# Block inverses of a chunked delta rule written straight into the tile of M, without mask, expansion and the intermediate W

## The chip, the cores and the metric

The kernel runs on one core of one Trainium2 chip, in float32. The metric is the device time of one execution in microseconds. The five engines are called as in the profile: PE (TensorE; its weight loads are PEld), DVE (VectorE), ACT (ScalarE), POOL (GpSimd) and SP (SyncE, which here only issues DMAs). Each works through its own list of instructions in order, and waits on semaphores for what another one has to finish first.

## The reference, cut to what matters

One encoder layer on x (1 x 2048 x 1024): a norm, one projection, then two groups that read it. Group A is a gated delta rule, forward and backward, with 4 heads of 128; group B is windowed attention. Their outputs are concatenated, projected and added to x. The change lies in group A, in the inverse of a triangular matrix per chunk:

```python
m = jnp.where(strict, jnp.einsum('bhncd,bhnsd->bhncs', k_beta, k) * decay, 0.0)
t_inv = lax.linalg.triangular_solve(eye + m, jnp.broadcast_to(eye, m.shape),
                                    left_side=True, lower=True, unit_diagonal=True)
u = jnp.einsum('bhncs,bhnse->bhnce', t_inv, v * beta[..., None])
w = jnp.einsum('bhncs,bhnsd->bhncd', t_inv, k_beta * jnp.exp(g)[..., None])
...
_, o = lax.scan(step, state0, xs)          # chunk after chunk, forwards
bwd = flip(gated_delta_rule_chunked(flip(q), flip(k), flip(v), ...))
```

The reference uses chunks of 64; the kernel uses 16 chunks of 128, which gives the same function. So each of the 4 heads has 2 directions x 16 chunks = 32 inverses of a unit triangular 128x128 matrix.

## The kernel before, in words

Phase A (to about 840 us) makes the projections, the convolution and the attention and leaves its results in DRAM. Phase B does group A head by head, and both output projections. For a head h it has these parts:

- `pre_front(h)`: for each of four groups `c4` of four chunks it loads keys and queries (`kq`), transposes them (`tr`), multiplies them (`gh`, two products of 256 columns per chunk), and DVE scales the products by decay (`dc`) and beta (`bp`) into the tile `ma[d, c4]` (L666). `ma[:, c, 0]` is M of chunk c, `ma[:, c, 1]` the matrix for the queries. `ssk` and `nk` are norms of the keys: squares on ACT, then DVE, then a power on POOL (L647). M goes to DRAM (`m_d`).
- the solve, at the head of `pre_back(h)`: the 32x32 blocks on the diagonals of all 32 matrices come back as one tile `L` (128 rows = 32 matrices x 4 blocks), and DVE inverts them together in 31 steps of two operations (L701, L705), each of which needs the one before. The result X goes to DRAM (`x_d`).
- the inverses, in the loop over `hi`: four pairs, group hi of direction 0 and group 3-hi of direction 1. For each group `xc` brings the inverted blocks, one 128x32 strip per chunk. POOL spreads each strip over 128 columns and multiplies it with the 0/1 mask `blk`, which leaves the block-diagonal matrix `xd` (L716); DVE transposes it 32x32 block by block into `xt` (L720). One of them is the right side x0 of the product `pb` = M x0 (L725), the other, x1, is the start of the iteration. ACT copies the blocks of `pb` off the diagonal into B (`bm`, L731, three copies). Then three times: a product `pw` = B W on PE (L737), and W = x1 - `pw` on DVE, 128x512 (L742). The third result is written over M, in `ma[:, :, 0]`.
- `scan(h)`: 16 steps, each for both directions: `pk`, `r`, `py` (the product with the inverse in `ma`), `yk` and `y` on ACT, `po` (three products), the new state `S` and the output `oacc`. Step i of direction 0 takes chunk i, of direction 1 chunk 15-i, so the first four steps need the first pair of inverses alone. `post` then norms the outputs (`sso`, `tro`, `zt`).

The order of all this is not that of the code: `set_order` plans the whole program. It takes every instruction with a cost by engine, shape and kind and a delay from one engine to the next, plays the program forwards and backwards twelve times by list scheduling, and fixes each engine's list as in the best plan. So the solve and the inverses of head h+1, and the front of head h+2, stand between the steps of scan h. The names in the lists are those above with head, direction and group: `pb2_1_3` is `pb` of head 2, direction 1, group 3. PE's products in float32 are two instructions each.

## Time and profile before

| | us |
|---|---|
| median of 3 runs | 1356.98 (1355.6 to 1359.8) |
| profiled execution, its own time | 1359.47 |
| its span in the profile | 1357.7 |
| PE busy | 1286.7 (95%) |
| DVE busy | 945.8 (70%) |
| ACT busy | 689.1 (51%) |
| POOL busy | 414.3 (31%) |

The profiled execution is 2.5 us above the median, and its span 1.8 us below its own time. "Busy" is the time in which an instruction of the engine was under way. The matmul instructions overlap each other in the profile, since each is listed with its whole passage through the engine, so PE's 95% leaves room that only the spacing of starts shows. In the rows of groups, waits and timeline, L with a number is a line of the kernel before; "<-" behind a time names what ended the wait.

### The profile page before, as it was taken

How to read it: one execution, taken by the hardware profiler on the slowest of the kernel's cores; microseconds unless marked ns; L12 is line 12 of the kernel's file. 1: busy time of each engine (PE TensorE's matmuls, PEld its weight loads, DVE VectorE, ACT ScalarE, POOL GpSimd, SP SyncE). 2: the span in 40 equal slices, each digit the busy share in tenths (PEclk: the TensorE clock that was granted, in tenths of full speed). 3: DMA queues.
4: the chain of work that ended last, by engine and by line, in shares of the span. 5: the costliest groups of instructions: out<-in, count | busy, mean ns of one | idle time of the engine just before them, and what ended most of it. 6: DMA issues, size and time to landing. Idle time of an engine off the chain costs nothing. (4 is left out here: it accounts for less than half of the span.)

```text
span 1357.7 us, 23034 instructions
## 1 busy us (share of the span) xinstructions
PE 1286.7 (95%) x7546; PEld 1106.8 (82%) x7546; DVE 945.8 (70%) x2346; ACT 689.1 (51%) x2025; POOL 414.3 (31%) x562
## 2 busy tenths in 40 slices
PE   5999989999999999999999899999979989999998
PEld 4998778788998888888887677789868869898776
DVE  4322477774632499999997797868898979977532
ACT  6322254332433466767667876129577575465310
POOL 1330062100121246657777644014034041120000
PEclk9999999999999999999999899999999999999999
DMA  8342255244434533223333658968476383332776
GB/s 263 112 132 91 74 162 170 68 132 137 150 119 119 164 104 109 64 86 96 99 127 118 216 179 255 286 193 240 112 211 167 87 226 85 96 104 87 235 246 209
DMA packets 219831, 201.26 MB, mean 148 GB/s; under 512 B 48320, under 2 KB 170944, under 8 KB 219712
## 3 DMA queue, kind: packets, MB, share of 16 engines
q1 hardware_dynamic: 219712, 199.79, 48.5%
q8 instruction: 60, 0.98, 0.3%
q14 instruction: 59, 0.48, 0.1%
HBM read 134.66 MB, written 65.08 MB: 147 GB/s over the span
## 5 line engine op out<-in xcount | busy, mean ns | idle before, releaser
L185 PE MATMUL pf_c<-xhi,wh_c 128*128 128x512 f32 x384 | 150.6, 403 | 5.4 <-DVE acc L236 5.4
L236 DVE SCALAR_TENSOR_TENSOR acc<-pf_c,cw,acc 128x512 f32<-128x512 f32 (+1 forms) x192 | 140.1, 743 | 21.8 <-ACT acc L232 20.2
L186 PE MATMUL pf_c<-xlo,wh_c 128*128 128x512 f32 x384 | 150.3, 402 | 0.0
L187 PE MATMUL pf_c<-xhi,wl_c 128*128 128x512 f32 x384 | 148.3, 399 | 0.0
L354 POOL TENSOR_SCALAR pr<-pr,st 128x384 f32<-128x384 f32 (+1 forms) x128 | 86.3, 691 | 35.6 <-DVE st L352 23.7
L186 PE MATMUL pf_z<-xlo,wh_z 128*128 128x512 f32 x256 | 93.7, 398 | 0.0
L185 PE MATMUL pf_z<-xhi,wh_z 128*128 128x512 f32 x256 | 93.5, 398 | 0.0
L187 PE MATMUL pf_z<-xhi,wl_z 128*128 128x512 f32 x256 | 93.0, 398 | 0.0
L185 PEld LDWEIGHTS pf_c<-xhi,wh_c 128*128 128x128 f32 x384 | 72.7, 189 | 21.0 <-DVE acc L236 5.3
L345 ACT ACTIVATE pr<-pr,st 128x384 f32<-128x384 f32 (+1 forms) x128 | 76.2, 597 | 26.6 <-DVE st L344 25.3
L187 PEld LDWEIGHTS pf_c<-xhi,wl_c 128*128 128x128 f32 x384 | 72.6, 189 | 14.6
L186 PEld LDWEIGHTS pf_c<-xlo,wh_c 128*128 128x128 f32 x384 | 72.7, 190 | 13.9
L359 PE MATMUL pt<-ident,pr 128*128 128x128 f32 x368 | 73.2, 281 | 8.0 <-POOL pr L354 5.3
L340 DVE CUSTOM_DVE_ANT_0 pr<-s,mask,sink 128x384 f32<-128x384 f32 (+1 forms) x128 | 72.8, 592 | 8.4 <-PE s L339 4.9
L716 POOL TENSOR_TENSOR xd<-xc,blk 128x512 f32<-128x512 f32 x32 | 41.3, 1300 | 120.3 <-DMA xc<-x_d 59.7
L737 PE MATMUL pw<-W,bm 128*128 128x128 f32 x512 | 73.4, 280 | 0.6 <-DVE W L742 0.4
L772 ACT ACTIVATE yk<-py,ck 128x128 f32<-128x128 f32 x120 | 43.7, 364 | 58.2 <-PE py L767 57.3
L363 ACT ACTIVATE ph<-pt 128x512 fp32r<-128x512 f32 x92 | 53.5, 594 | 38.1 <-PE pt L359 27.3
L359 PEld LDWEIGHTS pt<-ident,pr 128*128 128x128 f32 x368 | 49.1, 143 | 26.9 <-POOL pr L354 11.4
L364 DVE TENSOR_TENSOR pl<-pt,ph 128x512 fp32r<-128x512 f32 x92 | 62.2, 683 | 10.6 <-ACT ph L363 9.3
L737 PEld LDWEIGHTS pw<-W,bm 128*128 128x128 f32 x512 | 65.0, 194 | 2.8 <-DVE W L742 1.6
L177 DVE TENSOR_TENSOR wl_c<-ws_c,wh_c 128x512 fp32r<-128x512 f32 x48 | 36.1, 756 | 38.4 <-ACT wh_c L176 25.7
(244 smaller groups left out, 3776.7 us busy)
## 6 DMA issues: line engine op xcount, KB each, us to landing
kqc<-kq_d SPq DMA_DIRECT2D x120, 128.0 KB, 2.6
ws_c<-wt SPq DMA_DIRECT2D x48, 256.0 KB, 3.5
xr<-x SPq DMA_DIRECT2D x16, 512.0 KB, 5.9
ws_z<-wt SPq DMA_DIRECT2D x32, 256.0 KB, 3.6
kq<-kq_d SPq DMA_DIRECT2D x16, 512.0 KB, 5.0
xrs<-x SPq DMA_DIRECT2D x32, 256.0 KB, 3.9
part<-xrs SPq DMA_DIRECT2D x32, 256.0 KB, 3.5
m_d<-ma SPq DMA_DIRECT2D x32, 256.0 KB, 4.9
```

The lines of the kernel that those rows point to most:

```text
L185: T.matmul(ps, hi[:, k, cs], xhi[b][:, k], start=(k == 0), stop=False)
L186: T.matmul(ps, hi[:, k, cs], xlo[b][:, k], start=False, stop=False)
L187: T.matmul(ps, lo[:, k, cs], xhi[b][:, k], start=False, stop=(k == KC - 1))
L236: V.scalar_tensor_tensor(av, ps[:, lo:], cw[:, i, k : k + 1], av, ALU.mult, ALU.add)
L340: V.tensor_tensor_reduce(pr[j][:, :n], ps[:, :n], mask[:, lo * P : hi * P], 1.0, sink[:, hh : hh + 1], ALU.add, ALU.max, accum_out=mx[:, j ...
L345: A.activation(pr[j][:, :n], pr[j][:, :n], AF.Exp, bias=nm[:, j : j + 1], accum_out=den[:, j : j + 1])
L354: G.tensor_scalar(pr[j][:, :n], pr[j][:, :n], den[:, j : j + 1], 1.0, ALU.mult, ALU.mult)
L359: T.transpose(pt[:, j], pr[j][:, (kb - lo) * P : (kb - lo + 1) * P], ident)
L363: A.activation(ph, ptf, AF.Copy)
L364: V.tensor_tensor(pl, ptf, ph.bitcast(F32), ALU.subtract)
L737: T.matmul(pw_[:, c], B[:, c], wt[d][:, c], start=True, stop=True)
L772: A.activation(yk, py, AF.Copy, scale=ck[:, d, c : c + 1])
```

## The change

The mask `blk`, the expanded tiles `xd` and `xt` of 128x512 per group and the tiles W are gone. In their place:

- four tiles `xz` (two per direction, like B) are set to zero once. Of a strip x0, only the three blocks that `pb` needs are copied into the diagonal of `xz`, by POOL, as three copies of 32 partitions x 4 x 32.
- DVE transposes the strip itself (128x128 per group instead of 128x512).
- ACT writes B negated (`scale=-1.0`).
- POOL copies the four diagonal blocks x1 into the tile of M, once `pb` has read M.
- the three products read that tile itself instead of W. After product k only the blocks at distance k from the diagonal are new, and only they are written back into it: three copies on ACT after product 1, two on DVE after product 2, one on DVE after product 3.

```diff
-    NXB, NW = 3, 2
     XE = V
-    blk = const("blk", [P, P], t["blk"], qp)
     bms = [[const(f"bm{d}_{i}", [P, 4, P], None, qp) for i in range(2)] for d in range(2)]
-    for grp in bms:
+    xds = [[const(f"xz{d}_{i}", [P, 4, P], None, qp) for i in range(2)] for d in range(2)]
+    for grp in bms + xds:
         for a in grp:
             G.memset(a, 0.0)
...
-                xd = qp.tile([P, 4, P], F32, tag="xd", name=f"xd{h}_{d}_{c4}", bufs=NXB)
-                xt = qp.tile([P, 4, P], F32, tag="xt", name=f"xt{h}_{d}_{c4}", bufs=NXB)
-                B = bms[d][xcount[0] // 2 % 2]
+                k = xcount[0] // 2 % 2
+                B, xd = bms[d][k], xds[d][k]
                 xcount[0] += 1
                 xc = qp.tile([P, 4, 32], F32, tag="xc", name=f"xc{h}_{d}_{c4}", bufs=3)
+                xt = qp.tile([P, 4, 32], F32, tag="xt", name=f"xt{h}_{d}_{c4}", bufs=3)
                 dma(xc, x_d[d, 4 * c4 : 4 * c4 + 4].rearrange("u i c -> i u c"))
-                G.tensor_tensor(
-                    xd.rearrange("p u (q c) -> p u q c", q=4), xc.unsqueeze(2).to_broadcast([P, 4, 4, 32]),
-                    blk.rearrange("p (q c) -> p q c", q=4).unsqueeze(1).to_broadcast([P, 4, 4, 32]), ALU.mult,
-                )
-                V.transpose(xt.rearrange("p c i -> p (c i)"), xd.rearrange("p c i -> p (c i)"))
-                prs.append((d, c4, B) + ((xd, xt) if d == 0 else (xt, xd)))
+                V.transpose(xt.rearrange("p u c -> p (u c)"), xc.rearrange("p u c -> p (u c)"))
+                x0, x1 = (xc, xt) if d == 0 else (xt, xc)
+                for q in quads[d : d + 3]:
+                    G.tensor_copy(xd[q, :, q], x0[q])
+                prs.append((d, c4, B, xd, x1))
...
-                    A.activation(B[r, :, q], pb[r, :, q], AF.Copy)
-            wt = {d: x1 for d, c4, B, x0, x1 in prs}
-            for k in range(3):
+                    A.activation(B[r, :, q], pb[r, :, q], AF.Copy, scale=-1.0)
+                for q in quads:
+                    G.tensor_copy(ma[d, c4][q, :, 0, q], x1[q])
+            for k in range(1, 4):
                 for d, c4, B, x0, x1 in prs:
+                    m = ma[d, c4]
                     pw_ = ps_i[d].tile([P, 4, P], F32, tag="inv", name=f"pw{h}_{d}_{c4}_{k}")
                     for c in range(4):
-                        T.matmul(pw_[:, c], B[:, c], wt[d][:, c], start=True, stop=True)
-                    if k < 2:
-                        wt[d] = qp.tile([P, 4, P], F32, tag="W", name=f"W{h}_{d}_{c4}_{k}", bufs=NW)
-                    else:
-                        wt[d] = ma[d, c4][:, :, 0]
-                    V.tensor_tensor(wt[d], x1, pw_, ALU.subtract)
+                        T.matmul(pw_[:, c], B[:, c], m[:, c, 0], start=True, stop=True)
+                    for p in range(4 - k):
+                        r, q = (quads[p], quads[p + k]) if d == 0 else (quads[p + k], quads[p])
+                        if k == 1:
+                            A.activation(m[r, :, 0, q], pw_[r, :, q], AF.Copy)
+                        else:
+                            V.tensor_copy(m[r, :, 0, q], pw_[r, :, q])
```

Since the plan is made anew, the lists differ far beyond these lines, on PE from the second half of phase A on. Three places, all at the passage from scan 1 to scan 2, show what moves. In the lists of after, the lines behind the change are one lower or higher (L760 is now L761, L666 is L665, L742's place is taken by L743, L725 by L723, L716 by L718 and L731).

The first is DVE's list where the solve of head 2 ends (`X2`, L705, now L704). Before:

```order
L760 SCALAR_TENSOR_TENSOR r1_0_14_11911<-pk1_0_14_11909,negc_5022,vs1_3_10933 128x128
L779 SCALAR_TENSOR_TENSOR S1_1_13_11902<-S1_1_12_11816,egt_5024,po1_1_13_11894 128x128
L795 SCALAR_TENSOR_TENSOR oacc1_3_11337<-po1_0_13_11874,egc_5026,oacc1_3_11337 128x128
L666 SCALAR_TENSOR_TENSOR ma3_1_0_13601<-gh3_0_0_13634,bp3_13429,dc3_0_1_13598 128x256
L760 SCALAR_TENSOR_TENSOR r1_1_14_11931<-pk1_1_14_11929,negc_5022,vs1_0_10855 128x128
L795 SCALAR_TENSOR_TENSOR oacc1_0_11324<-po1_1_13_11894,egc_5026,oacc1_0_11324 128x128
L796 TENSOR_TENSOR oacc1_3_11337<-po1_0_13_11874,oacc1_3_11337 128x128
L796 TENSOR_TENSOR oacc1_0_11324<-po1_1_13_11894,oacc1_0_11324 128x128
L666 SCALAR_TENSOR_TENSOR ma3_0_0_13597<-gh3_0_0_13634,bp3_13429,dc3_0_0_13594 128x256
L666 SCALAR_TENSOR_TENSOR ma3_1_0_13601<-gh3_0_0_13634,bp3_13429,dc3_0_1_13598 128x256
L779 SCALAR_TENSOR_TENSOR S1_0_14_11922<-S1_0_13_11882,egt_5024,po1_0_14_11914 128x128
L705 TENSOR_TENSOR X2_12346<-X2_12346,tm2_30_12441 128x31
```

Now:

```order
L761 SCALAR_TENSOR_TENSOR r1_0_12_11887<-pk1_0_12_11885,negc_5022,vs1_3_10987 128x128
L796 SCALAR_TENSOR_TENSOR oacc1_2_11600<-po1_0_11_11850,egc_5026,oacc1_2_11600 128x128
L797 TENSOR_TENSOR oacc1_1_11579<-po1_1_11_11870,oacc1_1_11579 128x128
L797 TENSOR_TENSOR oacc1_2_11600<-po1_0_11_11850,oacc1_2_11600 128x128
L813 TENSOR_SCALAR sso1_1_11923<-ssq1_10676 128x8
L700 TENSOR_TENSOR tm2_30_12543<-L2_12447,X2_12448 128x31
L743 COPY ma1_1_0_10847<-pw1_1_0_2_11396 32x4x32 x2
L704 TENSOR_TENSOR X2_12448<-X2_12448,tm2_30_12543 128x31
```

The last step of this solve stood behind step 14 of scan 1 and stands now behind step 11. For head 3 it went from step 11 to step 9 of scan 2, for head 1 from step 12 to step 13 of scan 0.

The second is PE's list at the first product with the inverted blocks of head 2. Before:

```order
L769 MATMUL po1_0_15_11954<-S1_0_14_11922,kqc1_0_15_11947 128x128
L785 MATMUL po1_0_15_11954<-y1_0_15_11957,ma1_0_3_10867 128x128
L769 MATMUL po1_1_15_11969<-S1_1_14_11942,kqc1_1_15_11962 128x128
L785 MATMUL po1_1_15_11969<-y1_1_15_11972,ma1_1_0_10793 128x128
L674 MATMUL trv3_3_13736<-ident_66,vt3_3_13670 128x128 x4
L657 MATMUL gh3_3_1_13723<-kq3_3_13668 128x256 x2
L725 MATMUL pb2_0_0_12457<-xd2_0_0_12445,ma2_0_0_12193 128x128 x4
L725 MATMUL pb2_1_3_12465<-xt2_1_3_12452,ma2_1_3_12275 128x128 x4
```

Now:

```order
L759 MATMUL pk1_0_14_12011<-S1_0_13_11984,kqc1_0_14_12009 128x128
L777 MATMUL po1_1_13_11996<-yk1_1_13_11999,ks1_0_10853 128x128
L786 MATMUL po1_0_13_11976<-y1_0_13_11981,ma1_0_3_10921 128x128
L723 MATMUL pb2_0_0_12561<-xz0_0_8568,ma2_0_0_12295 128x128
L768 MATMUL py1_0_14_12015<-r1_0_14_12013,ma1_0_3_10921 128x128
L723 MATMUL pb2_0_0_12561<-xz0_0_8568,ma2_0_0_12295 128x128
L759 MATMUL pk1_1_14_12031<-S1_1_13_12004,kqc1_1_14_12029 128x128
```

It stood behind the last product of scan 1; now its first half stands between the products of steps 13 and 14.

The third is POOL's list there. Before:

```order
L647 TENSOR_TENSOR nk3_13428<-ssk3_13427,pw_4992 128x4
L631 TENSOR_TENSOR dc3_3_1_13676<-dc3_3_1_13676,dmask_4984 128x512
L716 TENSOR_TENSOR xd2_0_0_12445<-xc2_0_0_12447,blk_8564 128x512
L716 TENSOR_TENSOR xd2_1_3_12451<-xc2_1_3_12453,blk_8564 128x512
L814 TENSOR_TENSOR sso1_0_11977<-sso1_0_11977,pw_4992 128x8
```

Now:

```order
L718 COPY xz0_0_8568<-xc2_0_0_12547 32x4x32 x3
L718 COPY xz1_0_8570<-xt2_1_3_12555 32x4x32 x3
L630 TENSOR_TENSOR dc3_3_0_13822<-dc3_3_0_13822,dmask_4984 128x512
L646 TENSOR_TENSOR nk3_13578<-ssk3_13577,pw_4992 128x4
L718 COPY xz0_1_8569<-xc2_0_1_12627 32x4x32 x2
L630 TENSOR_TENSOR dc3_3_1_13826<-dc3_3_1_13826,dmask_4984 128x512
L731 COPY ma2_0_0_12295<-xt2_0_0_12548 32x4x32 x4
L718 COPY xz0_1_8569<-xc2_0_1_12627 32x4x32
L731 COPY ma2_1_3_12377<-xc2_1_3_12554 32x4x32 x4
```

The last group of head 3's front (`dc3_3`, `nk3`) stood ahead of head 2's first blocks and stands now between them and the copies into the tile of M.

More of the change, by code (lines that the diff above doesn't have):

```diff
@@ L1182, in layout @@
     dmask = np.stack([np.where(le, f(0), f(NEG)), np.where(i >= j, f(0), f(NEG))], 1).astype(f)
-    blk = (i // 32 == j // 32).astype(f)
     r = {
@@ L1189, in layout @@
         "sinks": g["swa_sinks"][0], "ident": np.eye(P, dtype=f), "cs": cs, "smask": smask, "tri": tri,
-        "dmask": dmask, "blk": blk, "eye32": np.eye(32, dtype=f),
+        "dmask": dmask, "eye32": np.eye(32, dtype=f),
     }
```

## Prediction

> **What bounds the kernel now.** I read the windows by stage first, then the spacing of PE's starts in the timeline, then the timeline of one passage from scan to scan, then PE's waits. The change lies in phase B alone, between 905 us (first `pb`) and 1262 us (last scan step):
>
> ```profile
> core 0: us, PE busy (x) PEld busy (x) DVE busy (x) ACT busy (x) POOL busy (x), PEclk, DMA share, GB/s
> 905.00:1009.00 104.00, 93.99 (x702) 87.20 (x701) 88.61 (x273) 74.94 (x325) 29.82 (x25) 0.97 0.59 162
> 1028.00:1101.00 73.00, 69.05 (x536) 63.22 (x535) 66.93 (x214) 48.46 (x202) 14.59 (x13) 1.00 0.51 139
> 1123.00:1188.00 65.00, 62.66 (x492) 57.77 (x493) 61.30 (x190) 32.02 (x117) 10.74 (x8) 1.00 0.31 86
> 905.00:1262.00 357.00, 329.83 (x2540) 304.94 (x2539) 304.55 (x906) 226.60 (x914) 86.15 (x68) 0.99 0.51 140
> ```
>
> PE is busy 92% of the 357 us, DVE 85%, ACT 63%, POOL 24%. In the bodies of scans 1 and 2 (second and third row) DVE stands at 92 and 94%: two engines are nearly full side by side. How much of PE's time is work shows in its starts where nothing is late:
>
> ```profile
> 1052.41 1.06 PE L737 MATMUL pw<-W,bm 128*128 128x128 f32 x8
> 1053.31 0.39 PE L767 MATMUL py<-r,ma 128*128 128x128 f32 x2
> ...
> 1016.99 1.13 PE L657 MATMUL gh<-kq 128*128 128x256 f32 x4
> 1017.96 0.61 PE L737 MATMUL pw<-W,bm 128*128 128x128 f32 x4
> ```
>
> Eight instructions of 128 columns take 1053.31 - 1052.41 = 0.90, so 0.1125 each and 0.225 a product (two instructions); a `gh` product takes 0.97/2 = 0.485. 2540 instructions at 0.1125 make 286, and the some 92 of 256 columns add 92 x 0.13 = 12: PE has 298 us of work in 357, and loses 59. That is what can be won.
>
> **Where it is lost.** Part of it is the passage from one scan to the next. The chain is solve, DRAM and back, block matrix, `pb`, B, three products with a step on DVE between, first `py`. From scan 1 to scan 2 the timeline has:
>
> ```profile
> 1099.44 0.18 DVE L705 TENSOR_TENSOR X<-X,tm 128x31 f32<-128x31 f32 x1
> 1100.40 0.55 SPq L706 DMA_DIRECT2D x_d<-X  x1
> 1105.36 2.17 SPq L715 DMA_DIRECT2D xc<-x_d  x3
> 1108.30 2.50 POOL L716 TENSOR_TENSOR xd<-xc,blk 128x512 f32<-128x512 f32 x2 [5.75 <-DMA xc<-x_d]
> 1109.62 2.07 PE L725 MATMUL pb<-xd,ma 128*128 128x128 f32 x8 [2.13 <-POOL xd L716]
> 1111.73 1.15 ACT L731 ACTIVATE bm<-pb 32x128 f32<-32x128 f32 x3 [2.29 <-PE pb L725]
> 1121.17 0.39 PE L767 MATMUL py<-vs,ma 128*128 128x128 f32 x2
> ```
>
> So 21.6 us go by from the end of the solve (1099.6) to the first `py`. PE's list holds from `pk1_0_15`, which ran as the solve ended, to `pb2_0_0` 10 products, 5 `gh` and 7 transposes (one instruction each): 2.25 + 2.43 + 0.79 = 5.5 us; from there to `py2_0_0` 32 products and 8 transposes: 8.1. 13.6 of 21.6 are work, 8.0 are lost. The other two passages, by the same rows:
>
> ```profile
> 998.45 0.18 DVE L705 TENSOR_TENSOR X<-X,tm 128x31 f32<-128x31 f32 x1
> 1025.30 0.39 PE L767 MATMUL py<-vs,ma 128*128 128x128 f32 x2
> ...
> 1175.08 0.17 DVE L705 TENSOR_TENSOR X<-X,tm 128x31 f32<-128x31 f32 x1
> 1196.66 0.39 PE L767 MATMUL py<-vs,ma 128*128 128x128 f32 x2
> ```
>
> Scan 0 to 1: 26.7 us, in PE's list 21.7 of work, 5.0 lost. Scan 2 to 3: 21.4, 18.0 of work, 3.4 lost. The three lose 16.4. The rest is in the scans, where PE's waits name DVE and ACT about equally; idle that shows as such is less than the loss by starts, since matmuls overlap:
>
> ```profile
> PE gh L657 <- DVE ma L666: 5.3, 4, 3.0
> PE pb L725 <- POOL xd L716: 3.3, 2, 2.1
> PE tro L824 <- ACT oacc L821: 3.2, 6, 1.7
> PE tr L637 <- ACT ks L640: 2.3, 2, 1.9
> PE po L776 <- ACT yk L772: 2.3, 6, 0.6
> PE py L767 <- DVE r L760: 2.2, 6, 0.6
> ```
>
> **The change, part by part.** The rows for the prices:
>
> ```profile
> 905.00:1262.00 357.00, 65.05 (x96) 0.99 0.51 140
> ...
> L720 DVE STREAM_TRANSPOSE xt<-xd x32: 668/702/714, 901.0 to 1229.2; 128x512 f32<-128x512 f32 x32
> ...
> L783 DVE COPY S<-po x8: 248/286/291, 917.1 to 1200.5; 128x128 f32<-128x128 f32 x8
> ...
> L731 ACT ACTIVATE bm<-pb 32x128 f32<-32x128 f32 x32 | 8.6, 268 | 19.6 <-PE pb L725 18.7
> ...
> L716 POOL TENSOR_TENSOR xd<-xc,blk x32: 1262/1270/2109, 898.9 to 1216.9; 128x512 f32<-128x512 f32 x32
> ...
> L258 POOL COPY bd<-sgkv x16: 192/196/433, 31.4 to 381.5; 128x16 f32<-128x16 f32 x16
> ...
> L354 POOL TENSOR_SCALAR pr<-pr,st x128: 472/586/1803, 196.5 to 836.4; 128x384 f32<-128x384 f32 x112, 128x256 f32<-128x256 f32 x16
> ```
>
> DVE. It loses the 96 subtractions (first row, the windows of L742 alone: 65.05 us) and 32 transposes of 512 columns (22.5). It gains 32 transposes of 128 columns, which no row has: between 0.18 (a quarter) and 0.70, taken 0.28 as the copy of the same width, 9 us; and 96 copies of 128 columns from PSUM at 0.28, 27. Net 51 us less, 304.6 to 253 of 357, 71%.
>
> ACT. 96 more copies of 32x128 from PSUM at 0.268: 25.7 us, 63% to 71%. The sign in B costs nothing: the same instructions with another constant.
>
> POOL. 32 x 7 = 224 copies of 128 elements instead of 32 `xd`. A copy lies between 0.196 (16 elements) and 0.472 (fastest of 384); on the line between them 0.28. That is 63 us for 41, in an engine with 24% load. Four more memsets fall ahead of the first `xc`, where POOL has nothing else to do.
>
> PE. As many products of the same shapes, one operand read from `ma` instead of W: nothing. SP: one load of the mask less, at the start of phase B, hidden behind phase A.
>
> The chain of a pair, uncontended. Up to `pb`: three copies (0.84) for one `xd` (1.27), and for direction 1 a transpose of 0.28 for 0.70; about 0.5 won. From `pb` to the first product: four POOL copies (1.1) beside B's three on ACT (1.15 in the row above), so level where POOL is free. Then three copies on ACT (0.8), two (0.5) and one (0.28) on DVE for three subtractions of 0.68: 0.5 won. So the chain keeps its length, but gets fourteen POOL instructions a pair where it had two. What changes is what stands beside it.
>
> The passages. With DVE's list lighter the plan puts the end of solve 2 behind step 11 instead of 14. PE's list then holds 23 products, 5 `gh` and 20 transposes up to `pb2_0_0` (9.9 us) and 46, 6 and 18 from there to `py2_0_0` (15.3): 25.2 us of work over a chain that took 21.6. Scan 2 to 3: 10.8 + 14.2 = 25.0 over 21.4. Scan 0 to 1: 10.3 + 9.4 = 19.7 over a chain of 22 to 26.7 (its write of X waited longer). I put the losses at 0.5, 0.5 and 4 for 8.0, 3.4 and 5.0: **11 won**.
>
> In the scans, DVE's load falls from 85 to 71%. Its waits above (`gh`, `r`; 7.5 us, one `gh` wait of 1.2 counted in a passage already) and their hidden part should fall by some half: **4 won**, between 0 (PE next waits for ACT or itself) and 10.
>
> Against it: head 0 has no scan to hide behind, and PE's list between its `pb` and `py` loses 1.5 us of cover: **1.5**. ACT's waits (`tro`, `ks`, `yk`: 7.8 us) grow with its load by a quarter: **2**. POOL's copies stand in one list with `dc` and `nk`, so a pair can stand behind a wait for the front; where the passage has slack it hides it, at heads 0 and 1 I count 1 each: **2**, between -2 (the chain's 0.5 won at every head) and 19 (below). The Trainium skill (Perfetto Trace Analysis, "GPSIMD Engine Instruction") says that GpSimd is eight processors of 16 partitions each, with queues of their own; by that the copies of four blocks could run side by side, this 2 would be gone and the sum 10.5, which no row here can show.
>
> And POOL and DVE hold each other up. Two `xd` ran here from 1043.7 to 1046.2, and a solve step beside them took 1.04, where its neighbour in width has a mean of 0.265:
>
> ```profile
> 1043.72 2.50 POOL L716 TENSOR_TENSOR xd<-xc,blk 128x512 f32<-128x512 f32 x2 [10.91 <-PE pb L725]
> 1044.06 1.04 DVE L701 TENSOR_TENSOR tm<-L,X 128x87 f32<-128x87 f32 x1
> ...
> L701 DVE TENSOR_TENSOR tm<-L,X 128x87 f32<-128x87 f32 x6 | 3.2, 539 | 0.0
> ...
> L701 DVE TENSOR_TENSOR tm<-L,X 128x112 f32<-128x112 f32 x6 | 1.6, 265 | 0.0
> ```
>
> In its group of six steps the meetings cost 3.2 - 1.6 = 1.6 us, and few widths stand out like that; the new copies (42 in the three later pairs of a head, 11.8 us of POOL, for six `xd`, 7.6) should cost a little more: **1**. If every one met a step at the price of this one (0.78 for 1.27 of POOL), it would be (11.8 - 7.6) x 0.61 = 2.6 a solve and 8 for three heads; the lower end is 0.
>
> The Trainium skill (SBUF — State Buffer, "Who interferes with whom") has this as a lock: a DVE operation with two SBUF inputs and a GpSimd operation that reads SBUF keep each other out for a whole instruction. The single row agrees, the group says that it seldom comes to that. By the rule alone the upper end of 8 would stand, and the sum below would be 1.5.
>
> Sum: 11 + 4 - 1.5 - 2 - 2 - 1 = 8.5 us. The profiled execution took 1359.5, so 1351.0; the median of the runs is 2.5 lower: **1348.5 us**.
>
> **Rivals.** *POOL's list becomes the chain* (slower). At head 2 `nk3` and two `dc3_3` stand between the first blocks and `ma2_0_0`, whose copies the product `pw2_0_0_1` needs; `nk` has one of POOL's longest waits:
>
> ```profile
> POOL nk L647 <- DVE ssk L646: 85.7, 10, 35.1
> L240 POOL COPY edge<-acc x12: 186/186/1045, 166.2 to 297.1; 128x4 f32<-128x4 f32 x12
> ```
>
> From `tr3_3_0` to that product PE's list holds 7.6 us, and ACT's copy and four squares, `nk` (1.0), `dc` (1.3) and eight copies take about as long. The second row shows that a copy can take five times its least. At heads 2 and 3 it begins to tell when a copy, waits included, passes 0.28 + 3.6/14 = 0.54 us (3.6 is the slack of 25.2 over 21.6, 14 the copies of a pair), at heads 0 and 1 at once. At 0.65 a first pair costs 5.2 more, 5.2 at two heads and 1.6 at two: 13.6 against the 8.5, so 1362; at 0.75 it is 1368. Against it: half of all `xd` took no more than 1.27 (the row above), though most ran beside the solves.
>
> *Nothing* (within 0.3%, about what a measurement of this kernel can tell from no change). `pb2_0_0` now stands ahead of scan 1's last steps. If the round trip through DRAM is 3 us late, as at head 1, PE waits there with the rest of the scan behind it, and a passage's loss only moves. With 4 of the 11 left the sum is 1.5: 1355.5. The lock between POOL and DVE at its upper end gives the same time; of this rival's chance I give it a third.
>
> *DVE set the pace of the scans* (much faster). PE's work in the bodies of scans 1 and 2 is 536 x 0.1125 = 60.3 and 492 x 0.1125 = 55.4 of 73 and 65 us, at 92 and 94% of DVE. If its 51 us were on the path, half of the 59 goes: 1329 to 1335.
>
> **How the numbers follow.** The forecast, 1341 to 1353, has 0.43; much faster 0.16; nothing 0.14; slower 0.27. All of the forecast and of much faster lie below 1352.9, 0.3% under the median. The range runs from 1331, which leaves out half of the much faster cases (0.08), to 1365, which leaves out somewhat less than half of the slower ones (0.11).
>
> **What would show it.** Right: copies of L743 near 0.28, DVE's share of the same stage near 71%, no `pb` waiting over 1 us at heads 2 and 3, and the end of solve 2 well ahead of the last `pk` of scan 1, not at it. Wrong: POOL copies over 0.5 us from start to start, PE waiting at the first product (L737) for `ma` of POOL, `tro` or `po` waiting longer for ACT, or solve steps of 0.6 us beside copies. What would make the forecast wrong most surely is a scan that keeps its pace although DVE has room: then PE's lost time sits in the delays from engine to engine, and not in DVE's load.

## The result, and the profile after

| | us |
|---|---|
| changed kernel, median of 14 runs | 1360.01 (1357.56 to 1362.65) |
| kernel before, 14 runs beside them | 1358.87 (1355.60 to 1365.29) |
| ratio, 95% interval | 1.0007 (0.9993 to 1.0022) |
| forecast | 1348.5 (1331 to 1365) |
| profiled execution of the changed kernel, its own time | 1362.25 |
| its span in the profile | 1360.5 |

No change can be told. The time lies in the forecast's range, but the gain of 8.5 us that was forecast isn't there.

The loads moved much as priced. The changed kernel's window over the same stage (columns as in the prediction's: length, then busy time and instructions of PE, PEld, DVE, ACT, POOL):

```profile
905.00:1262.00 357.00, 332.75 (x2539) 308.20 (x2538) 264.76 (x900) 251.54 (x1008) 115.59 (x254) 0.98 0.51 141
```

and its groups by line (busy us, mean ns of one | idle before them):

```profile
L743 DVE COPY ma<-pw 32x128 f32<-32x128 f32 x96 | 27.5, 286 | 25.4 <-PE pw L737 23.8
L715 DVE STREAM_TRANSPOSE xt<-xc 128x128 f32<-128x128 f32 x32 | 9.6, 303 | 2.1 <-DMA xc<-x_d 1.9
L741 ACT ACTIVATE ma<-pw 32x128 f32<-32x128 f32 x96 | 25.7, 267 | 9.6 <-PE pw L737 8.4
L731 POOL COPY ma<-xt 32x128 f32<-32x128 f32 x64 | 19.5, 305 | 110.1 <-PE pb L723 108.0
L737 PE MATMUL pw<-ma,bm 128*128 128x128 f32 x768 | 115.3, 280 | 9.0 <-issue 3.8 <-DVE ma L743 1.8 <-POOL ma L731 1.4
```

DVE went from 304.6 to 264.8 (74%; 253 and 71% were forecast), ACT from 226.6 to 251.5, POOL from 86.2 to 115.6. New is the last row: the idle time of PE ahead of the products `pw` is 9.0 us. In the kernel before, the same view gives three groups for them:

```profile
L737 PE MATMUL pw<-W,bm 128*128 128x128 f32 x512 | 73.4, 280 | 0.6 <-DVE W L742 0.4
L737 PE MATMUL pw<-xt,bm 128*128 128x128 f32 x128 | 20.8, 280 | 0.7 <-ACT bm L731 0.6
L737 PE MATMUL pw<-xd,bm 128*128 128x128 f32 x128 | 20.2, 279 | 1.3 <-POOL xd L716 0.7 <-issue 0.6
```

Together 2.6. So DVE gave up 40 us, and PE waits 6 us longer ahead of its products; for 3.8 of the 9.0 ("issue") the profile shows nothing that PE waited for.

The passages, in the timeline of the changed kernel: the end of each solve (the step of 31 columns), the first `py` of heads 0 to 3, the last `pk`:

```profile
916.43 0.49 PE L768 MATMUL py<-vs,ma 128*128 128x128 f32 x2 [0.37 <-DVE ma L743]
1005.01 0.18 DVE L704 TENSOR_TENSOR X<-X,tm 128x31 f32<-128x31 f32 x1
1033.39 0.39 PE L768 MATMUL py<-vs,ma 128*128 128x128 f32 x2
1088.87 0.19 DVE L704 TENSOR_TENSOR X<-X,tm 128x31 f32<-128x31 f32 x1
1119.49 0.39 PE L768 MATMUL py<-vs,ma 128*128 128x128 f32 x2
1164.73 0.19 DVE L704 TENSOR_TENSOR X<-X,tm 128x31 f32<-128x31 f32 x1
1192.53 0.39 PE L768 MATMUL py<-vs,ma 128*128 128x128 f32 x2
1263.16 0.42 PE L759 MATMUL pk<-S,kqc 128*128 128x128 f32 x2
```

| passage | solve's end to first py | PE's work in it (prediction) | lost | forecast | before | granted clock, before and now |
|---|---|---|---|---|---|---|
| scan 0 to 1 | 28.2 | 19.7 | 8.5 | 4 | 5.0 | 1.00, 0.88 |
| scan 1 to 2 | 30.4 | 25.2 | 5.2 | 0.5 | 8.0 | 0.92, 1.00 |
| scan 2 to 3 | 27.6 | 25.0 | 2.6 | 0.5 | 3.4 | 1.00, 1.00 |
| sum | | | 16.3 | 5 | 16.4 | |

The granted clock is that of PE in the windows of these stretches. It fell in another passage in each of the two profiled executions, so the sums can't be compared to the tenth: by the share of the clock that was missing (0.12 of 28.2 us now, 0.08 of 21.6 before), an equal clock would take at most 3.4 us off the one and 1.7 off the other, an estimate that leaves some 2 us won of the 11 forecast.

Solves 2 and 3 do end 10.6 and 10.3 us earlier, as the order said, but the first `py` of head 2 comes 1.7 us earlier, that of head 3 4.1 us, and what is won there is gone by the end. From the first `py` of head 0 to the last `pk` it is 1263.16 - 916.43 = 346.7 us; before it was 346.4, by these rows:

```profile
914.29 0.39 PE L767 MATMUL py<-vs,ma 128*128 128x128 f32 x2
1260.73 0.42 PE L758 MATMUL pk<-S,kqc 128*128 128x128 f32 x2
```

### The profile page after: what moved, and what is told of

The parts are those of the page before. It is cut to its first block, busy times and chain, and to the rows that moved or that the text cites. A ratio compares the mean times of both kernels' runs of the same rounds, so it can differ in the third digit from the quotient of the medians.

```text
span 1360.5 us, 23367 instructions
## 1 busy us (share of the span) xinstructions
PE 1290.6 (95%) x7546; PEld 1107.8 (81%) x7546; DVE 907.1 (67%) x2346; ACT 715.4 (53%) x2121; POOL 444.1 (33%) x758
## 4 chain that ended last, share of the span: by engine, by line
PE 72%; DVE 10%; ACT 6%; DMA 5%; issue 4%; POOL 3%; SPq 1%; DVEq 0%; ACTq 0%; POOLq 0%
PE pf_c L185 6%; PE pf_c L186 5%; PE pf_c L187 5%; PE pw L737 5%; PE pf_z L186 4%; PE pf_z L185 4%; PE pf_z L187 4%; PE pt L359 2%; PE pq_q L196 2%; PE pq_q L197 2%; PE pq_q L198 2%; PE pcd L557 2%; PE py L768 2%; PE pcd L558 2%; PE pcd L556 2%
## 5 line engine op out<-in xcount | busy, mean ns | idle before, releaser
L737 PE MATMUL pw<-ma,bm 128*128 128x128 f32 x768 | 115.3, 280 | 9.0 <-issue 3.8
L737 PEld LDWEIGHTS pw<-ma,bm 128*128 128x128 f32 x768 | 99.3, 193 | 13.8 <-issue 4.3
L665 DVE SCALAR_TENSOR_TENSOR ma<-gh,bp,dc 128x256 f32<-128x256 f32 x128 | 56.4, 475 | 10.2 <-PE gh L656 8.1
```

Of the source, the lines that this page charges most:

```text
L665: V.scalar_tensor_tensor(ma[d, c4][:, c], gh[:, k], bp[:, d, cc : cc + 1], gms[d][:, c : c + 1].to_broadcast([P, 2, P]), ALU.mult, ALU.mult,)
L737: T.matmul(pw_[:, c], B[:, c], m[:, c, 0], start=True, stop=True)
```

## Experiments

Each ran beside the kernel before, on the same chip; its ratio is to that kernel, whose median was 1357.6 to 1359.8 in these series. The changed kernel's 1360.01 is from a series of its own; differences to it are given in us, and by the ratios where that changes the reading. The theories that the expectations weigh go by letters; B, for one, says that PE's lost time sits in the delays from engine to engine, F that any new order is worth some us either way.

**One part at a time, each in an order made anew**

The x1 copies on DVE:

```diff
-                    G.tensor_copy(ma[d, c4][q, :, 0, q], x1[q])
+                    V.tensor_copy(ma[d, c4][q, :, 0, q], x1[q])
```

> The 128 copies of the diagonal blocks into M's tile go from POOL to DVE; all else is the changed kernel. Theory A (the chain of a group from pb to its last product got longer, with POOL's four copies standing in it, and PE waits at the products): POOL's load falls by about 37 us, the copies still stand in the chain but behind DVE's shorter reaction, and the time falls from 1360 to 1354 to 1358. Theory B (DVE's room is not on the path, PE loses its time in the delays from engine to engine): DVE gets about 36 us back, from 74 to 84%, and nothing changes, 1358.5 to 1361.5. Theory C (DVE's room is worth what was forecast, and something else ate it): DVE's load back at 84% costs 3 to 6 us, 1363 to 1366.

Measured: 1368.07 us, 1.0075 (1.0059 to 1.0090). Beyond what any theory gave.

The same two lines left out:

> The 128 copies of the diagonal blocks into M's tile are left out, so the products read M's own unit block instead of the inverse's; the output is not the reference's. Theory A (these copies lengthen the chain from pb to the first product): the waits of PE at the products fall from about 15 us to under 10, and the time to 1348 to 1354. Theory B (delays from engine to engine, which this leaves as they are on the ACT branch): 1358 to 1361. Theory C (POOL's list was eaten by the copies): POOL falls from 116 to about 79 us, 1352 to 1356.

Measured: 1357.24 us, 0.9988 (0.9974 to 1.0002). Less was won than A or C expected, and more than B: all of POOL's x1 copies are worth some 3 us.

The products in place, with the old expansion (cut, and written as an edit of the changed kernel):

```diff
-                for q in quads[d : d + 3]:
-                    G.tensor_copy(xd[q, :, q], x0[q])
+                G.tensor_tensor(
+                    xd.rearrange("p u (q c) -> p u q c", q=4), xc.unsqueeze(2).to_broadcast([P, 4, 4, 32]),
+                    blk.rearrange("p (q c) -> p q c", q=4).unsqueeze(1).to_broadcast([P, 4, 4, 32]), ALU.mult,
+                )
+                V.transpose(xt.rearrange("p c i -> p (c i)"), xd.rearrange("p c i -> p (c i)"))
...
-                    G.tensor_copy(ma[d, c4][q, :, 0, q], x1[q])
+                    G.tensor_copy(ma[d, c4][q, :, 0, q], x1[q, :, q])
```

> Only one part of the change: the products in place and the new blocks put out, with the old expansion by the mask (one POOL operation a group) and the full transposes. DVE has about 13 us more than the changed kernel, POOL some 96 small copies fewer and 32 large operations more, 14 us more. Theory A (POOL's copies into M's tile and the further hops make the chain): they are all still here, 1359 to 1363. The rival that the seven small copies ahead of pb and behind it fill POOL's list: 1355 to 1358. The rival that the expansion was the part that won and the blocks the part that lost: 1364 to 1368.

Measured: 1355.64 us, 0.9979 (0.9964 to 0.9994). That is the range of the rival that the small copies fill POOL's list.

More work for DVE, read by nobody:

```diff
+                for j in range(4):
+                    xq = qp.tile([P, 4, 32], F32, tag="xq", name=f"xq{h}_{d}_{c4}_{j}", bufs=4)
+                    V.transpose(xq.rearrange("p u c -> p (u c)"), xc.rearrange("p u c -> p (u c)"))
```

> The changed kernel with four more DVE transposes of 128 columns a group (128 in all, about 0.3 us each, 38 us), whose results nobody reads: DVE's load goes back to the 85% it had before, with nothing added to any chain. Theory B (DVE's room is not on the path): 1358.5 to 1362. Theory C (DVE's room is worth the 4 us forecast or more, and something else ate it): 1364 to 1369.

Measured: 1362.23 us, 1.0033 (1.0018 to 1.0047). Between B and C.

The mask's multiplication back, the transposes of 128 columns kept (the first hunk above, with x0 for `xc` and no second transpose):

> The changed kernel, but the block-diagonal operand of pb is filled by one POOL multiplication by the mask for a group (as before the change, 1.27 us) and not by three POOL copies; the transposes stay at 128 columns and the products in place. The kernel with the old expansion and the full transposes (the in-place part alone) took 1355.6, the changed one 1360. Theory D (the three copies ahead of pb cost those 4 us: three instructions to start behind the transfer or the transpose, where one did): 1354 to 1357. Theory E (the transposes of 128 columns and what they free on DVE cost it, through the plan): 1359 to 1362. Theory F (a new plan is worth some us either way whatever the edit): anywhere from 1353 to 1364, with no relation to the parts.

Measured: 1364.14 us, 1.0048 (1.0025 to 1.0072). D would have it near 1355.6, E at most at 1362. The parts of the expansion don't add up, which leaves theory F, whose range it passes by 0.1.

**The planner's luck.** One number of the planner, in three kernels:

```diff
-LAG = {"PE": 205, "DVE": 140, "Activation": 160, "Pool": 120, "SP": 2400}
+LAG = {"PE": 190, "DVE": 140, "Activation": 160, "Pool": 120, "SP": 2400}
```

> The kernel before the change, with one number of the planner changed: the delay that it assumes behind a PE instruction is 190 ns in place of 205. Not one instruction is added or removed, only the order on the engines is another. Theory F (a new plan is worth some us either way): 1361 to 1368, since 205 may be a number that suits just this kernel. The others: within 1.5 us of 1359.

> The changed kernel with the same number of the planner at 190. Theory F: 1354 to 1365, differing from 1360 by over 2 us. The others: within 1.5 us of 1360.

> The kernel with the in-place part alone (1355.6) with the same number of the planner at 190. Theory F: its gain of 3 us over the kernel before was its plan's, 1357 to 1365. Theory D (the old expansion with the new products is the better pair of parts): 1354 to 1357.5, and below the changed kernel at the same number by 3 us or more.

| kernel | at 205 | at 190 | ratio at 190 |
|---|---|---|---|
| before | 1358.5 | 1367.66 | 1.0075 (1.0056 to 1.0094) |
| changed | 1360.01 | 1363.75 | 1.0042 (1.0026 to 1.0059) |
| in place alone | 1355.64 | 1365.13 | 1.0055 (1.0034 to 1.0075) |

Without one instruction added or taken away a kernel moves by 4 to 10 us, and the changed kernel comes out 3.9 us faster than the one before at 190 and 1.1 slower at 205. Much of it falls where no line of the change acts. The first `pb` of head 0, for the kernel before at 205 and at 190:

```profile
905.74 0.46 PE L725 MATMUL pb<-xd,ma 128*128 128x128 f32 x2
```

```profile
912.16 1.05 PE L725 MATMUL pb<-xd,ma 128*128 128x128 f32 x8
```

and for the changed kernel and the one with the in-place part alone:

```profile
908.49 0.72 PE L723 MATMUL pb<-xz,ma 128*128 128x128 f32 x5
```

```profile
904.47 0.72 PE L725 MATMUL pb<-xd,ma 128*128 128x128 f32 x5
```

Of the 9 us that the first two differ by, 6.4 are there already, and 4.0 of the 4.4 between the last two.

So F holds, and the five experiments above can't be read part by part. The ones that follow hold the order.

**The copies' rows, in the changed kernel's own order.** The traces showed something in the small copies. In the changed kernel (timeline; a row of x3 or x2 stands for copies in sequence):

```profile
1116.18 0.83 ACT L741 ACTIVATE ma<-pw 32x128 f32<-32x128 f32 x3
...
1141.24 0.30 DVE L743 COPY ma<-pw 32x128 f32<-32x128 f32 x1
1141.57 0.35 DVE L780 SCALAR_TENSOR_TENSOR S<-S,egt,po 128x128 f32<-128x128 f32 x1
...
1068.67 0.27 DVE L743 COPY ma<-pw 32x128 f32<-32x128 f32 x1
1068.87 0.33 DVE L780 SCALAR_TENSOR_TENSOR S<-S,egt,po 128x128 f32<-128x128 f32 x1
```

Three ACT copies of 0.267 take 0.83, so each starts 0.28 after the one before: no overlap. Behind the first DVE copy the state update S starts after 0.33, behind the second after 0.20. The second copy starts at row 0, like S (it is the first block of direction 0); the first copy starts in another block of 32 rows. The Trainium skill has a rule for this (VectorE: DVE Perf Modes, "Two Vector instructions with no wait between them"): an instruction is held, and starts only when every earlier Vector instruction has finished, if the start quadrant (a block of 32 partitions) of one of its inputs differs from where the last instruction that read the same memory started, or that of its output from where the last one that wrote it did. The trace agrees: where an instruction stood ready behind one of the 96 DVE copies, and both start at row 0, it starts 0.20 to 0.25 us after the copy (14 of 15, one at 0.29); in all other cases it is 0.28 to 0.33. ACT's copies behave alike: each starts 0.26 to 0.28 us after the one before it.

The planner gives these copies, from one start to the next, 60 + 0.86 x 128 = 170 ns on ACT and 70 + 1.04 x 128 = 203 on DVE, as for 128 rows.

```diff
-                            A.activation(m[r, :, 0, q], pw_[r, :, q], AF.Copy)
+                            A.activation(m[:, :, 0, q], pw_[:, :, q], AF.Copy)
...
-                            V.tensor_copy(m[r, :, 0, q], pw_[r, :, q])
+                            V.tensor_copy(m[:, :, 0, q], pw_[:, :, q])
```

> The changed kernel in exactly its own order on every engine; only the 192 copies from the products into M's tile take all 128 rows instead of 32, over the same columns, so the blocks beside the new ones are overwritten and the output is not the reference's. In the changed kernel's trace such a copy of 32 rows starts 0.28 us (ACT) and 0.29 to 0.30 us (DVE) after the one before it, its whole duration, and the instruction behind it waits for its end too, while copies of the same width over 128 rows let the next start after 0.158 (ACT, y) and 0.20 (DVE, oacc). Theory G (copies whose rows start in another block of 32 don't overlap with their neighbours, which takes 0.1 us a copy, in the chain of every group): they start 0.16 and 0.20 apart, the waits of PE at the products shrink by some 5 us, the time is 1350 to 1355. Theory B (PE's loss is in the delays from engine to engine, and the order is tight): 1358.5 to 1361.5.

Measured: 1348.03 us, 0.9925 (0.9908 to 0.9941): 12 us faster than the changed kernel (11 by the ratios), better than G expected. In the traces all engines run the same sequence of instructions as in the changed kernel. The timeline of this run:

```profile
1108.57 0.59 ACT L741 ACTIVATE ma<-pw 128x128 f32<-128x128 f32 x3
...
1131.92 0.29 DVE L743 COPY ma<-pw 128x128 f32<-128x128 f32 x1
1132.12 0.34 DVE L780 SCALAR_TENSOR_TENSOR S<-S,egt,po 128x128 f32<-128x128 f32 x1
```

and its groups by line:

```profile
L743 DVE COPY ma<-pw 128x128 f32<-128x128 f32 x96 | 25.3, 285 | 24.6 <-PE pw L737 21.1 <-ACT ma L741 2.2 <-issue 0.6
L741 ACT ACTIVATE ma<-pw 128x128 f32<-128x128 f32 x96 | 20.4, 279 | 9.4 <-issue 6.7 <-PE pw L737 2.0 <-POOL xz L718 0.3
```

A copy lasts about as long as before (0.285 for 0.286 us, 0.279 for 0.267), but three on ACT now take 0.59 instead of 0.83, and S starts 0.20 behind its copy instead of 0.33 (both pairs of rows are the same place in the same order). The landmarks of this run:

```profile
916.10 0.49 PE L768 MATMUL py<-vs,ma 128*128 128x128 f32 x2 [0.38 <-DVE ma L743]
1000.81 0.18 DVE L704 TENSOR_TENSOR X<-X,tm 128x31 f32<-128x31 f32 x1
1027.83 0.39 PE L768 MATMUL py<-vs,ma 128*128 128x128 f32 x2
1081.14 0.18 DVE L704 TENSOR_TENSOR X<-X,tm 128x31 f32<-128x31 f32 x1
1111.65 0.39 PE L768 MATMUL py<-vs,ma 128*128 128x128 f32 x2
1154.68 0.19 DVE L704 TENSOR_TENSOR X<-X,tm 128x31 f32<-128x31 f32 x1
1182.09 0.39 PE L768 MATMUL py<-vs,ma 128*128 128x128 f32 x2
1248.90 0.41 PE L759 MATMUL pk<-S,kqc 128*128 128x128 f32 x2
```

Up to head 0's first `py` nothing differs (916.1 and 916.4). From there on, with the granted clock of each stretch:

| stretch | changed kernel, us | clock | copies of 128 rows, us | clock |
|---|---|---|---|---|
| `py` of head 0 to `py` of head 1 | 117.0 | 0.96 | 111.7 | 0.98 |
| head 1 to head 2 | 86.1 | 1.00 | 83.8 | 1.00 |
| head 2 to head 3 | 73.0 | 1.00 | 70.4 | 1.00 |
| head 3 to the last `pk` | 70.6 | 0.95 | 66.8 | 1.00 |

That is 14 us, in every scan that has inverses beside it. The passages alone take 26.8, 30.3 and 27.2 us, 84.4 for 86.2, so 12 of the 14 lie outside of them. Not all of the 14 is the copies': the changed kernel's profiled execution lies 2.2 us above its median, and in the first and the last stretch its clock was lower, which by the missing share is worth up to some 6 us (an estimate); the two stretches at full clock differ by 2.3 and 2.6. Of the 12 us between the medians the clock accounts for less: its mean over the runs is 0.991 and 0.992, and among the 14 runs of the changed kernel 0.001 goes with some 0.7 us. Whether the other values in the tiles play a part in the clock isn't shown.

The same for one engine at a time:

> The changed kernel in its own order; only the 96 copies on ACT behind the first product take 128 rows (the output is not the reference's). All 192 so widened gave 1348.0, 12 below the changed kernel. Theory G for both engines: the part follows the time that the copies and what stands behind them no longer take, some 0.12 + 0.13/3 a copy on ACT and 0.1 + 0.12/2 on DVE, so about half here, 1353 to 1356. If it is DVE's copies alone: 1358.5 to 1361.

Measured: 1356.73 us, 0.9986 (0.9973 to 1.0000); 3.3 below the changed kernel.

> The changed kernel in its own order; only the 96 copies on DVE behind the second and third products take 128 rows (the output is not the reference's). Theory G for both engines: 1353 to 1356, and this gain and that of the ACT copies alone add up to the 12 us of both. If it is ACT's copies alone: 1358.5 to 1361.

Measured: 1352.56 us, 0.9957 (0.9942 to 0.9972); 7.4 below. DVE pays twice as much as ACT, and 3.3 + 7.4 = 10.7 come near the 12 of both together. By the ratios it is 3, 7 and 11; ACT's part, whose interval touches the changed kernel's (0.9993 to 1.0022), is hardly clear of the noise.

**Instructions and order exchanged**

PE's instructions are chained, ahead of the planning, in the sequence that they have in the other kernel (`row`):

```diff
+    row = [pes[j] for j in itertools.accumulate(map(int, steps))]
+    for a, b in zip(row, row[1:]):
+        nxt[a].append((b, 0))
+        prv[b].append((a, 0))
```

> The changed kernel's instructions, with PE held to the order that it had before the change (its products are the same and of the same number); the planner orders the other engines around it. Theory F (the order decides): like the kernel before, 1357 to 1362, with DVE lighter by some 40 us and nothing of it won. Theory C (DVE's room is worth what was forecast where the order doesn't eat it): 1351 to 1356. Theory G (the small copies make the chain longer than three subtractions did, with no new order to win it back): 1361 to 1368.

> The instructions of the kernel before, with PE held to the changed kernel's order. In that order the pairs of heads 2 and 3 begin earlier and stand among the scan before, planned for a DVE with 40 us more room. Theory F (the order decides): 1358 to 1363. Theory C (the room of DVE is what the new order needs): 1366 to 1375, as the solves and subtractions come late and PE stands behind them.

| | PE's order of before | PE's order of the changed kernel |
|---|---|---|
| instructions of before | 1358.9 | 1387.10, 1.0217 (1.0199 to 1.0236) |
| instructions of the changed kernel | 1371.88, 1.0106 (1.0087 to 1.0125) | 1360.0 |

Both went further than expected. In the traces PE's sequence is that of the other kernel, while the other engines' lists are planned anew. Held to PE's old order, the new instructions cost 13 us: G's direction, with twice the size. In the new order the old ones are 27 us worse than the new, in the direction of theory C and beyond its range: that order needs the room on DVE. It fits that the order adapted and won by it about what the copies lose, but that is argued: no run shows what holding a list costs by itself.

DVE's load given back without a new order for PE:

> The changed kernel with PE held to its own order and the 128 further DVE transposes of the earlier experiment (31 us of DVE, results read by nobody); there the planner had made a new order for them (1362.2). Theory B (DVE's room is worth little): 1359 to 1364. Theory C (DVE's room is worth 4 us and more): 1364 to 1372.

Measured: 1365.00 us, 1.0055 (1.0036 to 1.0074), 5 us above the changed kernel (6.5 by the ratios), for this load (a group by line), which raises DVE's busy time in the window from 264.8 to 282.8 us:

```profile
L718 DVE STREAM_TRANSPOSE xq<-xc 128x128 f32<-128x128 f32 x116 | 28.6, 283 | 1.8 <-DMA xc<-x_d 1.7
```

C holds, at its lower end. The other engines' lists were planned anew here too, and the profiled execution (1362.1) lies 2.9 us under the median, so where the 5 us fall isn't shown.

**An order that knows the copies, and wider copies**

The three lines are the planner's costs of ACT, DVE and POOL instructions:

```diff
+        part = o[0].ap[0][1] == 32 and eng != "PE"
...
-            return 60 + 0.86 * m + 85 * (scalars > 0) + 110 * (len(o) > 1)
+            return 60 + 0.86 * m + 85 * (scalars > 0) + 110 * (len(o) > 1) + 110 * part
...
-            return 70 + 1.04 * m + 55 * (scalars > 0) + 10 * (i.opcode == "ISA")
+            return 70 + 1.04 * m + 55 * (scalars > 0) + 10 * (i.opcode == "ISA") + 95 * part
...
-        return 150 + 1.02 * m
+        return 150 + 1.02 * m + 47 * part
```

> The changed kernel's instructions, with the planner told what its traces show: an ACT instruction on 32 rows occupies its engine 0.11 us longer than the planner assumed, a DVE one 0.095, a POOL copy 0.047. Only the order changes. Theory G: an order made with these durations leaves the room that the chain needs: 1352 to 1357. Theory F (any new order is worth some us either way): 1354 to 1368. Theory B: 1358 to 1362.

Measured: 1352.78 us, 0.9954 (0.9937 to 0.9970): 7 us won by the order alone. That is within the 4 to 10 us by which the planner's other number moved the kernels, though it made all three slower. PE's idle time ahead of the products fell from 9.0 to 5.7:

```profile
L737 PE MATMUL pw<-ma,bm 128*128 128x128 f32 x768 | 115.1, 282 | 5.7 <-DVE ma L743 3.0 <-ACT ma L741 1.7 <-POOL ma L731 0.5
```

> The kernel before the change, with the planner told the same durations (it has 96 copies of 32 rows, those of B on ACT). Theory F: 1354 to 1369, by luck. Theory G: it has few such copies, so little to win: 1356 to 1361; and the changed kernel with these numbers is faster than this one by 3 us or more.

Measured: 1365.09 us, 1.0052 (1.0035 to 1.0068). The kernel before loses 5 us (7 by the ratio), which F allows and G did not; with these numbers the changed one is 12 us faster.

Fewer and wider copies:

```diff
+                    if k == 1:
+                        for p in range(3):
+                            r, q = (slice(0, 32 * p + 32), quads[p + 1]) if d == 0 else (quads[p + 1], quads[p])
+                            A.activation(m[r, :, 0, q], pw_[r, :, q], AF.Copy)
+                    else:
+                        lo, hi = slice(0, P - 32 * k), slice(32 * k, P)
+                        r, q = (lo, hi) if d == 0 else (hi, lo)
+                        V.tensor_copy(m[r, :, 0, q], pw_[r, :, q])
```

> The changed kernel with fewer and wider copies into M's tile: for the second product one copy of 64 rows by 64 columns in place of two of 32 by 32 (32 DVE copies fewer), for the first product in direction 0 copies of 32, 64 and 96 rows that all start at row 0; the blocks they touch beside the new ones are either right already or written again later, so the output is the same. Theory G: DVE's step after the second product falls from 0.6 to 0.4 us and ACT's three copies of direction 0 overlap; 1353 to 1358. Theory F: 1353 to 1367. Theory B: 1358 to 1361.

Measured: 1351.93 us, 0.9948 (0.9928 to 0.9968), below all three ranges.

Both together, the longer times only for what doesn't start at row 0:

> The kernel with the wider and fewer copies (1351.9), with the planner told the longer times, for those alone that don't start at row 0, and 0.33 us for a POOL copy. Theory G: the two gains (8 and 7 us by themselves) overlap, 1345 to 1351. Theory F: 1348 to 1360.

Measured: 1350.37 us, 0.9946 (0.9926 to 0.9966). The gains overlap almost wholly; these three versions beat both kernels by 6 to 10 us. Each of them has a new order as well as its edit, so how much of a gain is the order's luck isn't separated.

## Why the prediction was wrong

**The passages** (11 won) is the term of the sum that failed: 0.1 us was won. The step was "PE's list then holds 25.2 us of work over a chain that took 21.6", taken to leave a loss of 0.5. It takes PE's work off the chain's length, as if all of it lay beside the chain. The work is there, but most of it ahead of the chain's second half and not beside it. From the changed kernel's timeline, scan 1 to 2:

```profile
1100.09 0.39 PE L723 MATMUL pb<-xz,ma 128*128 128x128 f32 x2
1100.71 0.39 PE L723 MATMUL pb<-xz,ma 128*128 128x128 f32 x2
1106.58 0.83 PE L723 MATMUL pb<-xz,ma 128*128 128x128 f32 x6
1107.94 1.27 POOL L731 COPY ma<-xt 32x128 f32<-32x128 f32 x4
1110.70 0.46 PE L737 MATMUL pw<-ma,bm 128*128 128x128 f32 x2 [0.88 <-issue]
1114.19 2.02 PE L737 MATMUL pw<-ma,bm 128*128 128x128 f32 x16 [1.50 <-issue]
1117.06 2.05 PE L737 MATMUL pw<-ma,bm 128*128 128x128 f32 x16 [0.53 <-ACT ma L741]
```

`pb` begins 9.5 us earlier than before, but its third product stands behind scan 1's last steps and runs at 1106.6. In the 12.9 us from there to `py` (1119.5) the trace has 9.3 us of PE's work (65 instructions of 128 columns and 8 of 256, at the prediction's prices), so 3.7 us are lost there, 2.9 of them at the three waits ahead of the products; in the 17.5 us before, 1.9 are lost. At scan 0 to 1, 2.9 us go to one wait for DVE:

```profile
1016.21 1.13 PE L656 MATMUL gh<-kq 128*128 128x256 f32 x4 [2.92 <-DVE ma L665]
```

That a passage's loss only moves is the outcome of the rival "Nothing", but not its way: it had PE waiting at `pb` for the round trip, and PE's waits between 905 and 1262 us name no `pb`. The copies' hold isn't the reason either: with the same lists and copies of 128 rows the passages still lose 7.1, 5.1 and 2.2, 14.5 in all, so 1.9 of the 11 are won. One of the prediction's counts is off, too: in the kernel before, PE's instructions from scan 2 to 3 are 16.3 us of work in the trace and not 18.0. With all passages counted in the traces the losses are 18.2 before, 18.4 now and 16.9 without the hold.

**The scans** (4 won, between 0 and 10). DVE's room is worth something: load given back (18 us of busy time) cost 5 us. What was missing in the sum is a term of some 12 us on the other side: the 192 copies, most of which start in another block of rows than the instructions beside them, in the chain of every group and in the lists of the recurrence's steps. The prediction took their duration right (0.268 and 0.28 for 0.267 and 0.286) and saw the chain of a pair as no longer; it didn't compare the durations with those that the planner used to make the order that it read, and counted nothing for the instruction behind a copy. Without that hold, in the same order, the kernel takes 1348.0. That this is so near to the forecast of 1348.5 is chance: from head 0's first `py` to the last `pk` it is 13.6 us less than before the change, and of these the passages have 1.9, where 11 were forecast, and the scans 11.7 (in part by the clock), where 4 were. The 2.5 us that the forecast took off for the median rested on three runs, too: over 14 the kernel before has 1358.87, 0.6 below its profiled execution.

**ACT's waits** (2 lost): ACT's load came as forecast (70%, 71% forecast), but the waits did not grow with it. Of the three that the term was made of, 7.8 us before, 3.5 are left:

```profile
PE tr L636 <- ACT ks L639: 1.7, 4, 0.7
PE tro L825 <- ACT oacc L822: 1.6, 3, 1.1
PE po L777 <- ACT yk L773: 0.2, 1, 0.2
```

**POOL's list** (2 lost): without the x1 copies 2.8 us less, though in another order. The rival "POOL's list becomes the chain" needed 0.54 us a copy; four take 1.27, about 0.33 from start to start, and it fell.

**The lock** (1 lost): no loss shows; the two operations of the solve, in windows of their lines, went from

```profile
905.00:1262.00 357.00, 34.26 (x93) 0.99 0.51 140
905.00:1262.00 357.00, 31.99 (x93) 0.99 0.51 140
```

to

```profile
905.00:1262.00 357.00, 31.12 (x93) 0.98 0.51 141
905.00:1262.00 357.00, 31.80 (x93) 0.98 0.51 141
```

3.3 us less. In the whole trace before, 18 operations of the solve overlap one on POOL and take 4.7 us more than the median of their width alone; in the changed kernel 52 do, and take 0.6 more. So meetings became more frequent and cheaper, and the upper end of 8 isn't borne out. **Head 0** (1.5 lost): its first `py` is 2.1 us later than before, but its first `pb` is 2.8 later already, and from `pb` to `py` it is 7.9 us for 8.6 (908.49 to 916.43, 905.74 to 914.29). The loss doesn't show.

Of the signs that were named, those for "right" came (copies near 0.28, DVE at 74%, no wait at `pb`, solve 2 well ahead of scan 1's end), though nothing was won: none of them looks at PE behind `pb`. Of those for "wrong" PE waiting at L737 came, though only 1.4 of the 9.0 us for POOL. The chance of 0.14 for no change was too small for one more reason: a new order of the whole program is worth 4 to 10 us by itself, as large as the effect, and the range had no term for it.

## What to carry to other kernels

Replacing one wide operation by copies of single blocks of 32 rows costs more than their durations say: see how soon the next instruction starts behind one, and let copies start at row 0, or cover more rows, where the blocks beside are written again anyway. Where a planner orders the program, put the new operations' measured times into it before the edit is judged, and judge it over more than one order: holding the order (same sequence, one size changed) told in one run what five edits with new orders couldn't. Work that an order moves ahead of a chain doesn't cover the chain.

## What the runs showed of the hardware

- A copy from PSUM of 128 columns takes DVE as long for 128 rows (0.285 us) as for 32 (0.286), but the next instruction starts after 0.20 where both start at row 0 and after 0.28 to 0.33 where the block of the start row changes. From copy to copy on ACT it is 0.16 to 0.17 against 0.26 to 0.28. Whether the tile read or the tile written decides was not separated.
- POOL's copies of four different blocks of 32 rows don't run side by side (four in 1.27 us). The Trainium skill (Perfetto Trace Analysis, "GPSIMD Engine Instruction") says that GpSimd is eight processors with queues of their own; the overlap that the prediction weighed by it doesn't show here.
- The granted clock isn't even over an execution, and it fell in different stretches of the two that were profiled: from scan 0 to 1 it was 1.00 before the change and 0.88 after it, from scan 1 to 2 it was 0.92 and 1.00.
